# A four-mixer layer on one core: another order for the same instructions

## The chip, the core and the metric

The kernel runs on one core of a Trainium2 chip. The metric is the device time of one execution in microseconds (us), lower is better. The core has five engines that run their own queues in order: PE (matmuls, with its weight loads shown as PEld), DVE and ACT (vector and scalar work), POOL (a third elementwise engine) and SP, which issues the transfers.

## The reference, cut to what matters

One layer over 2048 positions of width 1024: normalise, project to four mixers, run them side by side, project back, normalise and add.

```python
h = _rmsnorm(x, pre_norm_w)
proj = jnp.einsum('btd,de->bte', h, w_in)              # 1024 -> 4120
p_gdn, p_rwkv, p_sc, p_gla = _split(proj, [...])
y_gdn = _gated_deltanet(p_gdn, ...)                    # chunks of 64, a triangular solve per chunk
y_rwkv = _rwkv7(p_rwkv, ...)                           # a recurrence over positions
y_sc = _short_conv(p_sc, sc_conv_w)
y_gla = _gla(p_gla, ...)                               # chunks of 64, a decayed state
y = jnp.concatenate([y_gdn, y_rwkv, y_sc, y_gla], axis=-1)
out = jnp.einsum('bte,ed->btd', y, w_out)
x = x + _rmsnorm(out, post_norm_w)
```

Each of the deltanet, rwkv and gla has four heads and a state that is carried from one chunk of 64 positions to the next, so their chunks follow one another.

## The kernel before, in words

The sequence is cut into 4 blocks of 512 positions. For each block the main thread `projections` multiplies 31 weight tiles (128 columns each) with the normalised input. A tile takes 24 matmuls of 128x512, since weights and input are held as a high and a low part, into one of two PSUM banks called pp; an epilogue on ACT, DVE and POOL reads the bank. The order of tiles in a block is deltanet, rwkv, short convolution, gla. After block 4 the same thread does the output projection, `out_proj`.

The mixers run beside it as further threads, Python generators that issue a few operations and then yield:

- `prepare` makes, for each block, the deltanet's gates and norms, then the matrices of each tile of 128 positions; the same for rwkv (`rwkv_prep`, twice per block, once per pair of heads, with a long run of DVE and ACT operations from L867 to L889, then `rwkv_mats`); then `gla_prep`.
- `inverses` inverts the 64x64 triangular matrices, 8 chunk matrices at a time, 16 times in all. Each goes through levels: matmuls into the bank psi, a masked product W on DVE (L591), matmuls with Yb, a sum X (L596), a transpose Y (L598), block-diagonal copies Yb (L583).
- `chains` carries the states: `gdn_chain`, `rwkv_chain` and `gla`, with PSUM banks psc and psa; after a tile, `norm` normalises its output (L1069 to L1081) and a thread `put` gates and stores it.
- `stats` and `front` normalise the next block's input; `load_out` loads the output weights.

**How the order comes about.** There are two steps. First the program order: `weave` (L227) keeps a planner's time `self.t`, which only matmuls advance, and each thread's due time. A number that a thread yields is a delay from the table `LAT`; a tuple is an event to wait for. The main thread steps until `BEAT` (1.5 us of planner's time) has passed since the mixers last had their turn, then every thread that is due steps, again and again until none is due. Second, the tile scheduler takes the program and orders each engine's queue: it runs a model of the machine and hands each engine, whenever it is free in that model, the ready instruction that comes first by program position. `tc.high_priority(offset=n)` moves the operations inside it n positions ahead for that choice; it is used for weight loads, for the input's high and low parts, and for the epilogues of projections (400 each). It changes no dependence. On the chip each queue then runs in the order fixed so, whatever the real durations are.

Buffers tie the blocks together: the deltanet projections of a block wait for the deltanet outputs of the block before (`yield "G", blk - 1`), and the rwkv projections for the rwkv outputs (L1381):

```python
more[0] = (("R", blk - 1) if blk else None,) + more[0][1:]
```

Of the kernel before, what the change touches and what calls it, by code (L numbers as in the profile page):

```python
# [19 lines left out]
P = 128  # L20
# [105 lines left out]
class Ring:  # L126
# [6 lines left out]
    def __call__(self):  # L133
# [31 lines left out]
FPRIO = 400  # L165

BEAT = 1.5
RG = 4
BANKS = {"pp": 2, "psa": 3, "psi": 1, "psc": 2}

LAT = {"gates": 6.0, "ipre": 2.0, "gates2": 1.0, "norms": 3.2, "chan": 0.9, "pool": 1.38, "decay": 2.6, "mats": 2.2, "inv0": 1.0, "inv1": 2.2,
       "invr": 0.8, "chA": 1.0, "chB": 0.7, "chC": 0.48, "rpre": 5.0, "rchan": 4.5, "gpre": 3.0, "gA": 1.1,
       "gB": 0.62, "out": 8.0, "front": 0.3, "rdec": 0.6, "fdone": 2.0, "wo0": 2.8, "wo1": 1.4, "bonus": 2.5}
# [12 lines left out]


class K:
    def __init__(self, tc, a, out):
        self.tc, self.nc, self.a, self.out = tc, tc.nc, a, out  # L190
        self.t, self.left, self.ev, self.threads = 0.0, 0.0, {}, []

# [10 lines left out]
    def thread(self, gen, prio):  # L203
        self.threads.append([prio, 0.0, None, gen])
        self.threads.sort(key=lambda th: th[0])
# [11 lines left out]
    def step(self, th):  # L217

        y = next(th[3], "end")
        if y == "end":  # L220
            self.threads.remove(th)
        elif isinstance(y, tuple):
            th[2] = y
        else:
            th[1] = self.t + y

    def weave(self):  # L227

        while self.threads:
            main = self.threads[-1]
            ready = [th for th in self.threads if th[0] < 99 and self.can(th)]
            if main[0] == 99 and self.can(main) and (not ready or self.t - self.left < BEAT):
                self.step(main)
            elif ready:
                while ready:
                    for th in ready:
                        self.step(th)
                    ready = [th for th in self.threads if th[0] < 99 and self.can(th)]  # L240
                self.left = self.t
            else:
                if not any(self.can(th) for th in self.threads):
                    w = [th[1] for th in self.threads if th[2] is None]
                    assert w, [(th[0], th[2]) for th in self.threads]
                    self.t = max(self.t, min(w))
# [311 lines left out]
    def inverse(self, Bh, Bl, n):  # L558
# [9 lines left out]
        for c in range(2):  # L568
            nc.vector.tensor_copy(Bb[hs(c), :, hs(c)], Bh[hs(c)])

# [4 lines left out]
        Y = self.R16["Y"]()  # L575
        nc.vector.tensor_tensor(Y, Bh, m4(self.n1t), ALU.mult)
        nc.vector.tensor_tensor(Y, Y, I16, ALU.add)
        X = self.R16["X"]()
        nc.vector.transpose(X, Y)
        def diag():  # L580
            Yb = self.Rbd["Yb"]()
            for c in range(2):
                nc.vector.tensor_copy(Yb[hs(c), :, hs(c)], Y[hs(c)])  # L583
            return Yb
        Yb = diag()
        yield LAT["ipre"]
        for lv in range(4):
            ps = self.psi()
            mmb(ps, Bb, X)
            W = self.R16["W"]()  # L590
            nc.vector.tensor_tensor(W, v(ps), m4(self.lev[lv]), ALU.mult)  # L591
            yield LAT["inv0"]
            ps = self.psi()
            mmb(ps, Yb, W)
            X2 = self.R16["X"]()
            nc.vector.tensor_tensor(X2, v(ps), X, ALU.add)  # L596
            X = X2
            nc.vector.transpose(Y, X)  # L598
            Yb = diag()
            yield LAT["inv0"] if lv == 3 else LAT["inv1"]  # L600
        ps = self.psi()
        mmb(ps, Bb, X)
        W = self.R16["W"]()
        nc.vector.tensor_tensor(W, v(ps), m4(self.lev[4]), ALU.mult)
        yield LAT["inv0"]
# [6 lines left out]
        X2 = self.R16["X"]()  # L612
        nc.vector.tensor_tensor(X2, v(px), X, ALU.add)
        nc.vector.tensor_tensor(Y, py, Y, ALU.add)
        X = X2

        T = self.R16["X"]()
        nc.vector.tensor_tensor(T, I16, X, ALU.subtract)
        yield LAT["invr"]
# [6 lines left out]
        R = self.R16["W"]()  # L626
        nc.vector.tensor_tensor(R, T, v(ps), ALU.subtract)
        yield LAT["inv0"]
# [6 lines left out]
        Yf = self.R["Yf"]()  # L635
        nc.vector.tensor_tensor(v(Yf), v(ps), Y, ALU.add)
        return v(Yf)
# [209 lines left out]
    def rwkv_prep(self, blk):  # L847
# [10 lines left out]
        for pr in range(2):  # L858
# [14 lines left out]
            nc.vector.memset(e[:, :, 0:1], 1.0)  # L873
            nc.scalar.activation(e[:, :, 1:65], c3(G), AF.Exp)
            ev = e.rearrange("p (a c) t -> p a c t", c=2)
            en, ak = self.t2(), self.t2()
# [5 lines left out]
            nc.vector.scalar_tensor_tensor(ak, av, 1.0, kk, ALU.add, ALU.mult)  # L882
            nc.vector.tensor_tensor(slot(bks, 0), c4(ak), c4(en), ALU.mult)
            nc.scalar.activation(av, av, AF.Identity, scale=self.d[:, 17 + pr:18 + pr], bias=self.d[:, 13 + pr:14 + pr])
            nc.vector.tensor_tensor(k_, k_, m3(av), ALU.mult)
            nc.vector.scalar_tensor_tensor(m3(add[:, pr, :]), r_, self.pcol("rk", pr), k_, ALU.mult, ALU.mult)
            nc.vector.tensor_tensor(k_, k_, m3(en), ALU.mult)
            nc.vector.tensor_tensor(slot(ars, 1), slot(ars, 1), ev[:, :, :, 1:65], ALU.mult)
# [82 lines left out]
    def gdn_chain(self, tt, m, Y):  # L971
# [5 lines left out]
        for cp in range(2):  # L977
# [3 lines left out]
            for pr in range(2):  # L981
                self.mm(pA[:, P * pr:P * pr + P], g["kqc"][pr][:, c, :], S[:, pr, :], start=True, stop=True)
            nc.vector.tensor_tensor(h4(D)[q], h4(pA[:, 0:256])[q], bc(g["ne1"])[q], ALU.mult)
            nc.vector.tensor_tensor(D[q], D[q], m["vT"][q], ALU.add)
            nc.vector.tensor_tensor(h4(t)[qn], h4(pA[:, 0:256])[qn], bc(g["e1s"])[qn], ALU.mult)
            n = 8 * cp + 2 * tt
            nc.vector.tensor_tensor(S, S, g["dec"][:, n:n + 2].unsqueeze(2).to_broadcast([P, 2, P]), ALU.mult)
            yield LAT["chA"]
# [4 lines left out]
            for hp in range(2):  # L993
                nc.scalar.copy(qh(w)[q, :, hp, :], pB[hs(hp), 0:P].rearrange("p (q d) -> p q d", q=2))  # L994
            yield LAT["chB"]
# [11 lines left out]
        for cp in range(2):  # L1007
            nc.vector.tensor_tensor(og[hs(cp)], t[hs(1 - cp)], pO[hs(1 - cp), 0:256], ALU.add)
        return og

    def add_state(self, S, pC):
        pv = pC[:, 0:P].rearrange("p (q d) -> p q d", q=2)
        for hp in range(2):
            sb = S[hs(hp), :, hs(hp)]
            self.nc.vector.tensor_tensor(sb, sb, pv[hs(hp)], ALU.add)

    def rwkv_chain(self, tt, m, Y):
# [11 lines left out]
        for cp in range(2):  # L1029
            c = 2 * tt + cp  # L1030
            q = hs(cp)
            for pr in range(2):
                self.mm(pAc[cp][:, P * pr:P * pr + P], r["AR"][pr][:, c, :], S[:, pr, :], start=False, stop=True, skip_group_check=True)
            nc.scalar.copy(D[q], pAc[cp][q])
            nc.vector.tensor_tensor(S, S, r["dec"][:, :, c:c + 1].to_broadcast([P, 2, P]), ALU.mult)
            yield LAT["chB"]
# [3 lines left out]
            for hp in range(2):  # L1040
                s = slice(4 * tt + hp, 4 * tt + hp + 3, 2)
                nc.vector.tensor_tensor(qh(uv[:, cp, :])[q, :, hp, :], pB[hs(hp), 0:P].rearrange("p (q d) -> p q d", q=2),  # L1042
                                        r["nkn"][hp == cp][hs(hp), s].unsqueeze(2).to_broadcast([64, 2, 64]), ALU.mult)
# [12 lines left out]
        for cp in range(2):  # L1056
            nc.scalar.copy(og[hs(cp)], pAc[cp][hs(1 - cp)])
        return og
# [165 lines left out]
    def gla_prep(self):  # L1224
# [7 lines left out]
        dec = self.R["ld"]()  # L1232
        nc.vector.tensor_copy(dec, c3(eb)[:, :, 63])
        nc.scalar.activation(en, G, AF.Exp, scale=-1.0 / 16)
        nc.vector.tensor_tensor(c3(ed), c3(G)[:, :, 63:64].to_broadcast([P, NC, 64]), c3(G), ALU.subtract)
        nc.scalar.activation(G, ed, AF.Exp, scale=1.0 / 16)
        nc.gpsimd.tensor_tensor(G, kf, G, ALU.mult)
        nc.vector.tensor_tensor(kf, kf, en, ALU.mult)
        L.update(ed=G, dec=dec)
# [9 lines left out]
    def gla(self, blk, tt):  # L1249
# [9 lines left out]
        ke, vt = kv[:, 0:P], kv[:, P:]  # L1259
        nc.vector.tensor_tensor(h4(at), h4(pa[:, 0:256]), self.incl.unsqueeze(1).to_broadcast([P, 4, 64]), ALU.mult)  # L1260
        pt = self.psa()
        for i, t in enumerate([L["ed"]] + L["v"]):
            self.tr(pt[:, i * P:(i + 1) * P], t[:, ts], self.ident)
        nc.scalar.copy(kv, pt[:, 0:3 * P])
        yield LAT["gA"]
# [11 lines left out]
        for cp in range(2):  # L1277
            c = 2 * tt + cp
            for h in range(4):
                self.mm(po[hs(cp), hs(h)], self.qbd[:, cp, h, :], self.Sl, start=False, stop=True, skip_group_check=True)  # L1280
            nc.vector.scalar_tensor_tensor(self.Sl, self.Sl, L["dec"][:, c:c + 1], pC[cp], ALU.mult, ALU.add)  # L1281
            if cp == 0:
# [5 lines left out]
        o = u1()  # L1288
        nc.scalar.copy(o, po[:, 0:256])
        self.norm(o, u1, EPS, False)  # L1290
# [144 lines left out]
```

## Time and profile before

| | |
|---|---|
| median of 3 runs | 1380.93 us (1374.62 to 1382.09) |
| profiled execution, time | 1382.66 us |
| profiled execution, span | 1380.9 us |
| instructions | 25696 |
| PE busy | 1286.0 us, 93% |
| PEld busy | 974.5 us, 71% |
| DVE busy | 966.9 us, 70% |
| ACT busy | 532.1 us, 39% |
| POOL busy | 357.1 us, 26% |

The span runs from the first to the last instruction; the profiled execution's own time holds 1.8 us more. Busy shares are means over stages that differ: the first 35 us load and split weights, the middle mixes projections with the four mixers, and from about 1265 us on only the output projection is left. Names such as W, Yb, psi or gu are the program's tiles, and L591 is line 591 of the kernel before. Matmuls overlap one another, so a row's mean duration is longer than the time from one matmul to the next.

### The profile page before, as it was taken

The numbers are of one execution on the slowest core, as the hardware profiler recorded it, in microseconds if no ns is written. First come the engines' busy times: TensorE is split into PE (matmuls) and PEld (weight loads), VectorE is DVE, ScalarE is ACT, GpSimd is POOL, SyncE is SP. The second block draws the span as 40 slices with busy tenths as digits, with TensorE's granted clock in tenths as the row PEclk, the third lists the DMA queues.
The fourth block names the chain that finished last, engine by engine and source line by source line (L and its number), as shares of the span: only waits on it lengthen the run. The fifth ranks groups of instructions, "written<-read, shape, count | busy, mean of one in ns | idle before, by whom it ended". The sixth has DMA issues, their size and how long they took to land. (4 is left out here: it accounts for less than half of the span.)

```text
span 1380.9 us, 25696 instructions
## 1 busy us (share of the span) xinstructions
PE 1286.0 (93%) x9928; PEld 974.5 (71%) x9928; DVE 966.9 (70%) x2194; ACT 532.1 (39%) x1165; POOL 357.1 (26%) x437
## 2 busy tenths in 40 slices
PE   5989988899999999999999899999998998999997
PEld 3767766667767777767677677676776776777886
DVE  5776697778886787688757894888669847643222
ACT  4653454235442441435524422453234234232221
POOL 5564443301121121111311211103112144232221
PEclk9999999999999999999999999999999998999999
DMA  7876554453244424453444333532444362233442
GB/s 278 272 253 228 206 176 145 142 167 121 92 139 136 155 93 151 140 177 123 139 145 137 123 126 130 165 125 93 146 134 142 117 213 87 93 111 100 150 151 99
DMA packets 98506, 204.47 MB, mean 148 GB/s; under 512 B 9152, under 2 KB 39248, under 8 KB 98384
## 3 DMA queue, kind: packets, MB, share of 16 engines
q1 hardware_dynamic: 98384, 202.83, 44.6%
q8 instruction: 78, 1.28, 0.4%
q14 instruction: 44, 0.36, 0.1%
HBM read 153.51 MB, written 49.28 MB: 147 GB/s over the span
## 5 line engine op out<-in xcount | busy, mean ns | idle before, releaser
L197 PE MATMUL pp<-hh,w 128*128 128x512 f32 (+1 forms) x2272 | 642.2, 408 | 7.9 <-ACT hh L432 4.0
L197 PEld LDWEIGHTS pp<-hh,w 128*128 128x128 f32 (+1 forms) x2272 | 413.0, 190 | 96.8 <-issue 5.1
L197 PE MATMUL pp<-hl,w 128*128 128x512 f32 (+1 forms) x1152 | 340.7, 408 | 2.0 <-POOL hl L433 2.0
L197 PEld LDWEIGHTS pp<-hl,w 128*128 128x128 f32 (+1 forms) x1152 | 209.3, 190 | 47.3 <-POOL hl L433 3.8
L350 POOL TENSOR_TENSOR w<-raw,w 128x512 fp32r<-128x512 f32 (+1 forms) x102 | 129.2, 1270 | 222.1 <-ACT w L349 121.6
L354 POOL TENSOR_TENSOR sm<-sm,mhalf 128x4 f32<-128x4 f32 (+1 forms) x64 | 59.7, 933 | 221.7 <-DVE sm L1077 196.0
L349 ACT CAST w<-raw 128x512 fp32r<-128x512 f32 (+1 forms) x102 | 60.4, 594 | 132.2 <-issue 60.9
L197 PE MATMUL pp<-woh,w 128*128 128x512 f32 x256 | 73.8, 409 | 0.0
L659 DVE SCALAR_TENSOR_TENSOR pq<-pq,par,pq 128x512 f32<-128x512 f32 x72 | 59.0, 819 | 14.7 <-ACT pq L656 12.3
L583 DVE COPY Yb<-Y 64x512 f16<-64x512 f16 x160 | 57.2, 358 | 2.2
L197 PEld LDWEIGHTS <-Yb 128*128 128x128 f16 x640 | 24.9, 99 | 44.5 <-issue 18.7
L197 PE MATMUL psi<-W,Yb 128*128 128x64 f16 x640 | 33.1, 196 | 23.5 <-DVE W L591 16.9
L197 PEld LDWEIGHTS pp<-woh,w 128*128 128x128 f32 x256 | 48.0, 193 | 9.5
L596 DVE TENSOR_TENSOR X<-psi,X 128x512 f16<-128x512 f32 x64 | 43.9, 686 | 9.6 <-PE psi L197 9.2
L197 PEld LDWEIGHTS <-Bb 128*128 128x128 f16 x768 | 29.6, 99 | 27.2 <-issue 21.6
L1368 DVE SCALAR_TENSOR_TENSOR pq<-pq,sm,x 128x512 f32<-128x512 f32 x32 | 24.0, 751 | 31.1 <-DMA x<-in_x 20.6
L598 DVE STREAM_TRANSPOSE Y<-X 128x512 f16<-128x512 f16 x64 | 45.2, 706 | 0.9
L1357 ACT ACTIVATE x<-pp 128x512 f32<-128x512 f32 x32 | 19.1, 598 | 68.8 <-PE pp L197 68.8
L591 DVE TENSOR_TENSOR W<-psi,c 128x512 f16<-128x512 f32 x64 | 43.6, 682 | 1.7 <-PE psi L197 1.2
L197 PE MATMUL psi<-X,Bb 128*128 128x64 f16 x768 | 39.7, 195 | 4.1 <-DVE X L596 3.6
L994 ACT COPY gu<-psc 64x128 f32<-64x128 f32 x64 | 16.7, 260 | 59.0 <-PE psc L197 58.0
L1358 DVE TENSOR_TENSOR pq<-pp,lg 128x512 f32<-128x512 f32 x16 | 11.1, 691 | 36.2 <-ACT x L1357 36.2
(317 smaller groups left out, 2087.2 us busy)
## 6 DMA issues: line engine op xcount, KB each, us to landing
w<-parts SPq DMA_DIRECT2D x186, 512.0 KB, 3.3
parts<-w SPq DMA_DIRECT2D x62, 512.0 KB, 4.0
raw<-in_wt SPq DMA_DIRECT2D x62, 256.0 KB, 3.1
x<-in_x SPq DMA_DIRECT2D x56, 256.0 KB, 3.0
raw<-yd SPq DMA_DIRECT2D x32, 256.0 KB, 2.9
out<-pq SPq DMA_DIRECT2D x32, 256.0 KB, 2.1
x<-in_xt SPq DMA_DIRECT2D x24, 256.0 KB, 2.9
yd<-y SPq DMA_DIRECT2D x32, 128.0 KB, 2.0
```

What stands on the lines that cost most here:

```text
L197: return self.nc.tensor.matmul(out, w, x, **kw)
L349: self.nc.scalar.copy(hi, src)
L350: self.nc.gpsimd.tensor_tensor(lo, src, hi.bitcast(F32), ALU.subtract)
L354: self.nc.gpsimd.tensor_tensor(dst, x, self.mhalf[:, 0:x.shape[1]], ALU.pow)
L583: nc.vector.tensor_copy(Yb[hs(c), :, hs(c)], Y[hs(c)])
L591: nc.vector.tensor_tensor(W, v(ps), m4(self.lev[lv]), ALU.mult)
L596: nc.vector.tensor_tensor(X2, v(ps), X, ALU.add)
L598: nc.vector.transpose(Y, X)
L659: nc.vector.scalar_tensor_tensor(acc, p[:, i:i + BL], self.pcol("conv", 4 * ct + i), acc, ALU.mult, ALU.add)
L994: nc.scalar.copy(qh(w)[q, :, hp, :], pB[hs(hp), 0:P].rearrange("p (q d) -> p q d", q=2))
L1357: nc.scalar.activation(junk, ps[i], AF.Square, accum_out=ss[:, i:i + 1])
L1368: nc.vector.scalar_tensor_tensor(o, o, r, x, ALU.mult, ALU.add)
```

## The change

The same arithmetic is issued in another order.

- The tile scheduler uses its timeline model instead of its default one to order the queues (`schedule_with_timeline_sim=True`).
- A wrapper `Urgent` issues an operation with a priority offset of 800. `self.uv` wraps DVE and `self.ua` wraps ACT; the inverse's DVE operations, and the chains' DVE and ACT operations that lie on the states' way, go through them.
- `rwkv_prep` yields three times inside its run of operations (0.5 us each by the planner) and its closing delay falls from 5.0 to 1.0; `gla_prep` yields twice.
- In `weave`, a thread that has yielded a positive delay takes no second step in the same visit.

```diff
+URGENT = 800
-       "invr": 0.8, "chA": 1.0, "chB": 0.7, "chC": 0.48, "rpre": 5.0, "rchan": 4.5, "gpre": 3.0, "gA": 1.1,
+       "invr": 0.8, "chA": 1.0, "chB": 0.7, "chC": 0.48, "rpre": 1.0, "burst": 0.5, "rchan": 4.5, "gpre": 3.0, "gA": 1.1,
+class Urgent:
+    def __init__(self, tc, eng):
+        self.tc, self.eng = tc, eng
+    def __getattr__(self, name):
+        op = getattr(self.eng, name)
+        def f(*a, **kw):
+            with self.tc.high_priority(offset=URGENT):
+                return op(*a, **kw)
+        return f
+        self.uv, self.ua = Urgent(tc, tc.nc.vector), Urgent(tc, tc.nc.scalar)
 # step
             th[1] = self.t + y
+            if y > 0.0:
+                th[4] = self.visit
 # weave
             elif ready:
+                self.visit += 1
                 while ready:
                     for th in ready:
                         self.step(th)
-                    ready = [th for th in self.threads if th[0] < 99 and self.can(th)]
+                    ready = [th for th in self.threads if th[0] < 99 and self.can(th) and th[4] < self.visit]
 # inverse (all its DVE operations likewise)
-            nc.vector.tensor_tensor(W, v(ps), m4(self.lev[lv]), ALU.mult)
+            self.uv.tensor_tensor(W, v(ps), m4(self.lev[lv]), ALU.mult)
 # rwkv_prep
             nc.scalar.activation(e[:, :, 1:65], c3(G), AF.Exp)
+            yield LAT["burst"]
...
             nc.vector.tensor_tensor(slot(bks, 0), c4(ak), c4(en), ALU.mult)
+            yield LAT["burst"]
...
             nc.vector.scalar_tensor_tensor(m3(add[:, pr, :]), r_, self.pcol("rk", pr), k_, ALU.mult, ALU.mult)
+            yield LAT["burst"]
 # gdn_chain, rwkv_chain, add_state and gla (their operations on D, t, S, w, uv, og, at, kv, Sl, o likewise)
-            nc.vector.tensor_tensor(h4(D)[q], h4(pA[:, 0:256])[q], bc(g["ne1"])[q], ALU.mult)
+            self.uv.tensor_tensor(h4(D)[q], h4(pA[:, 0:256])[q], bc(g["ne1"])[q], ALU.mult)
-                nc.scalar.copy(qh(w)[q, :, hp, :], pB[hs(hp), 0:P].rearrange("p (q d) -> p q d", q=2))
+                self.ua.copy(qh(w)[q, :, hp, :], pB[hs(hp), 0:P].rearrange("p (q d) -> p q d", q=2))
 # gla_prep
         nc.vector.tensor_copy(dec, c3(eb)[:, :, 63])
+        yield LAT["burst"]
...
         nc.gpsimd.tensor_tensor(G, kf, G, ALU.mult)
+        yield LAT["burst"]
 # kernel
-    with tile.TileContext(nc) as tc:
+    with tile.TileContext(nc, schedule_with_timeline_sim=True) as tc:
```

## Rows read from the trace of the kernel before

**Rows 1.** Page, busy us (share of the span) by engine, and instructions.

```profile
PE 1286.0 (93%) x9928; PEld 974.5 (71%) x9928; DVE 966.9 (70%) x2194; ACT 532.1 (39%) x1165; POOL 357.1 (26%) x437
```

**Rows 2.** Stretches: length, PE, PEld, DVE, ACT, POOL, clock, DMA, GB/s.

```profile
0.00:35.00 35.00, 19.31 (x73) 13.42 (x74) 17.95 (x43) 17.20 (x36) 20.64 (x27) 1.00 0.80 280
175.00:210.00 35.00, 27.72 (x162) 20.91 (x160) 33.19 (x52) 17.17 (x29) 17.65 (x14) 0.90 0.49 170
...
245.00:280.00 35.00, 29.97 (x232) 22.64 (x232) 26.94 (x54) 10.25 (x21) 8.23 (x9) 0.90 0.47 159
1295.00:1330.00 35.00, 35.00 (x156) 28.98 (x155) 10.01 (x19) 8.81 (x22) 9.62 (x9) 1.00 0.44 147
1365.00:1381.00 16.00, 8.39 (x38) 6.60 (x36) 4.49 (x8) 1.38 (x4) 0.55 (x1) 0.87 0.30 106
```

**Rows 3.** Chain that ended last, in time: start us, us, what.

```profile
1276.35 97.06 PE pp L197 x428
```

**Rows 4.** Page, instruction groups: xcount, busy us, mean ns, idle before.

```profile
L197 PE MATMUL pp<-hh,w 128*128 128x512 f32 (+1 forms) x2272 | 642.2, 408 | 7.9 <-ACT hh L432 4.0
```

**Rows 5.** PE's waits, by what ended them: total us, times, longest.

```profile
PE psi L197 <- DVE W L591: 16.9, 11, 4.8
...
PE psc L197 <- DVE gu L984: 8.1, 11, 2.9
PE psa L201 <- DVE or L1081: 4.5, 4, 2.6
PE psi L197 <- DVE Yb L583: 4.3, 7, 0.9
...
PE psi L197 <- DVE X L596: 3.6, 5, 2.1
PE psa L197 <- DVE t L779: 3.4, 1, 3.4
PE psc L197 <- DVE UV L1042: 3.1, 5, 0.8
PE pp L197 <- DMA w<-parts: 2.4, 3, 1.2
```

**Rows 6.** Timeline, DVE and PE, 182 to 188.6: start us, us, instruction.

```profile
182.95 2.77 DVE L583 COPY Yb<-Y 64x512 f16<-64x512 f16 x2
185.75 0.69 DVE L896 TENSOR_REDUCE n<-t 128x8 f32<-128x512 f32 x1
186.36 1.22 DVE L871 TENSOR_TENSOR_SCAN t<-c,t 128x512 f32<-128x512 f16 x1
187.50 0.68 DVE L591 TENSOR_TENSOR W<-psi,c 128x512 f16<-128x512 f32 x1
...
188.24 0.58 PE L197 MATMUL psi<-W,Yb 128*128 128x64 f16 x8 [4.79 <-DVE W L591]
```

**Rows 7.** Groups of DVE by line, whole span.

```profile
L591 DVE TENSOR_TENSOR W<-psi,c 128x512 f16<-128x512 f32 x64 | 43.6, 682 | 1.7 <-PE psi L197 1.2
```

**Rows 8.** Cores: span and mean granted clock.

```profile
core 0: 1380.9 us, clock 0.979
```

**Rows 9.** Timeline, the operation L1077 twice and POOL beside the first.

```profile
242.34 1.30 POOL L1237 TENSOR_TENSOR lg<-lqk,lg 128x512 f32<-128x512 f32 x1
242.44 1.22 DVE L1077 TENSOR_SCALAR sm<-sm 128x4 f32<-128x4 f32 x1
...
678.52 0.16 DVE L1077 TENSOR_SCALAR sm<-sm 128x4 f32<-128x4 f32 x1
```

**Rows 10.** Timeline, ACT: rwkv chain's last copies, projections' first epilogues.

```profile
373.90 0.59 ACT L825 COPY pq<-pp 128x512 f32<-128x512 f32 x1
383.77 0.75 ACT L1057 COPY or<-psc 64x256 f32<-64x256 f32 x2 [3.75 <-PE psc L197]
...
660.02 0.74 ACT L1057 COPY or<-psc 64x256 f32<-64x256 f32 x2 [1.65 <-PE psc L197]
...
673.62 0.57 ACT L825 COPY pq<-pp 128x512 f32<-128x512 f32 x1
```

More of the change, by code (lines that the diff above doesn't have):

```diff
@@ L190, in __init__ @@
         self.tc, self.nc, self.a, self.out = tc, tc.nc, a, out
-        self.t, self.left, self.ev, self.threads = 0.0, 0.0, {}, []
+        self.uv, self.ua = Urgent(tc, tc.nc.vector), Urgent(tc, tc.nc.scalar)
+        self.t, self.left, self.visit, self.ev, self.threads = 0.0, 0.0, 0, {}, []
     def mm(self, out, w, x, **kw):
@@ L203, in thread @@
     def thread(self, gen, prio):
-        self.threads.append([prio, 0.0, None, gen])
+        self.threads.append([prio, 0.0, None, gen, 0])
         self.threads.sort(key=lambda th: th[0])
@@ L568, in inverse @@
         for c in range(2):
-            nc.vector.tensor_copy(Bb[hs(c), :, hs(c)], Bh[hs(c)])
+            self.uv.tensor_copy(Bb[hs(c), :, hs(c)], Bh[hs(c)])
         def mmb(ps, l, r):
@@ L575, in inverse @@
         Y = self.R16["Y"]()
-        nc.vector.tensor_tensor(Y, Bh, m4(self.n1t), ALU.mult)
-        nc.vector.tensor_tensor(Y, Y, I16, ALU.add)
+        self.uv.tensor_tensor(Y, Bh, m4(self.n1t), ALU.mult)
+        self.uv.tensor_tensor(Y, Y, I16, ALU.add)
         X = self.R16["X"]()
-        nc.vector.transpose(X, Y)
+        self.uv.transpose(X, Y)
         def diag():
@@ L582, in diag @@
             for c in range(2):
-                nc.vector.tensor_copy(Yb[hs(c), :, hs(c)], Y[hs(c)])
+                self.uv.tensor_copy(Yb[hs(c), :, hs(c)], Y[hs(c)])
             return Yb
@@ L595, in inverse @@
             X2 = self.R16["X"]()
-            nc.vector.tensor_tensor(X2, v(ps), X, ALU.add)
+            self.uv.tensor_tensor(X2, v(ps), X, ALU.add)
             X = X2
-            nc.vector.transpose(Y, X)
+            self.uv.transpose(Y, X)
             Yb = diag()
@@ L603, in inverse @@
         W = self.R16["W"]()
-        nc.vector.tensor_tensor(W, v(ps), m4(self.lev[4]), ALU.mult)
+        self.uv.tensor_tensor(W, v(ps), m4(self.lev[4]), ALU.mult)
         yield LAT["inv0"]
@@ L612, in inverse @@
         X2 = self.R16["X"]()
-        nc.vector.tensor_tensor(X2, v(px), X, ALU.add)
-        nc.vector.tensor_tensor(Y, py, Y, ALU.add)
+        self.uv.tensor_tensor(X2, v(px), X, ALU.add)
+        self.uv.tensor_tensor(Y, py, Y, ALU.add)
         X = X2
         T = self.R16["X"]()
-        nc.vector.tensor_tensor(T, I16, X, ALU.subtract)
+        self.uv.tensor_tensor(T, I16, X, ALU.subtract)
         yield LAT["invr"]
@@ L626, in inverse @@
         R = self.R16["W"]()
-        nc.vector.tensor_tensor(R, T, v(ps), ALU.subtract)
+        self.uv.tensor_tensor(R, T, v(ps), ALU.subtract)
         yield LAT["inv0"]
@@ L635, in inverse @@
         Yf = self.R["Yf"]()
-        nc.vector.tensor_tensor(v(Yf), v(ps), Y, ALU.add)
+        self.uv.tensor_tensor(v(Yf), v(ps), Y, ALU.add)
         return v(Yf)
@@ L982, in gdn_chain @@
                 self.mm(pA[:, P * pr:P * pr + P], g["kqc"][pr][:, c, :], S[:, pr, :], start=True, stop=True)
-            nc.vector.tensor_tensor(h4(D)[q], h4(pA[:, 0:256])[q], bc(g["ne1"])[q], ALU.mult)
-            nc.vector.tensor_tensor(D[q], D[q], m["vT"][q], ALU.add)
-            nc.vector.tensor_tensor(h4(t)[qn], h4(pA[:, 0:256])[qn], bc(g["e1s"])[qn], ALU.mult)
+            self.uv.tensor_tensor(h4(D)[q], h4(pA[:, 0:256])[q], bc(g["ne1"])[q], ALU.mult)
+            self.uv.tensor_tensor(D[q], D[q], m["vT"][q], ALU.add)
+            self.uv.tensor_tensor(h4(t)[qn], h4(pA[:, 0:256])[qn], bc(g["e1s"])[qn], ALU.mult)
             n = 8 * cp + 2 * tt
-            nc.vector.tensor_tensor(S, S, g["dec"][:, n:n + 2].unsqueeze(2).to_broadcast([P, 2, P]), ALU.mult)
+            self.uv.tensor_tensor(S, S, g["dec"][:, n:n + 2].unsqueeze(2).to_broadcast([P, 2, P]), ALU.mult)
             yield LAT["chA"]
@@ L1007, in gdn_chain @@
         for cp in range(2):
-            nc.vector.tensor_tensor(og[hs(cp)], t[hs(1 - cp)], pO[hs(1 - cp), 0:256], ALU.add)
+            self.uv.tensor_tensor(og[hs(cp)], t[hs(1 - cp)], pO[hs(1 - cp), 0:256], ALU.add)
         return og
@@ L1014, in add_state @@
             sb = S[hs(hp), :, hs(hp)]
-            self.nc.vector.tensor_tensor(sb, sb, pv[hs(hp)], ALU.add)
+            self.uv.tensor_tensor(sb, sb, pv[hs(hp)], ALU.add)
     def rwkv_chain(self, tt, m, Y):
@@ L1033, in rwkv_chain @@
                 self.mm(pAc[cp][:, P * pr:P * pr + P], r["AR"][pr][:, c, :], S[:, pr, :], start=False, stop=True, skip_group_check=True)
-            nc.scalar.copy(D[q], pAc[cp][q])
-            nc.vector.tensor_tensor(S, S, r["dec"][:, :, c:c + 1].to_broadcast([P, 2, P]), ALU.mult)
+            self.ua.copy(D[q], pAc[cp][q])
+            self.uv.tensor_tensor(S, S, r["dec"][:, :, c:c + 1].to_broadcast([P, 2, P]), ALU.mult)
             yield LAT["chB"]
@@ L1041, in rwkv_chain @@
                 s = slice(4 * tt + hp, 4 * tt + hp + 3, 2)
-                nc.vector.tensor_tensor(qh(uv[:, cp, :])[q, :, hp, :], pB[hs(hp), 0:P].rearrange("p (q d) -> p q d", q=2),
+                self.uv.tensor_tensor(qh(uv[:, cp, :])[q, :, hp, :], pB[hs(hp), 0:P].rearrange("p (q d) -> p q d", q=2),
                                         r["nkn"][hp == cp][hs(hp), s].unsqueeze(2).to_broadcast([64, 2, 64]), ALU.mult)
@@ L1056, in rwkv_chain @@
         for cp in range(2):
-            nc.scalar.copy(og[hs(cp)], pAc[cp][hs(1 - cp)])
+            self.ua.copy(og[hs(cp)], pAc[cp][hs(1 - cp)])
         return og
@@ L1259, in gla @@
         ke, vt = kv[:, 0:P], kv[:, P:]
-        nc.vector.tensor_tensor(h4(at), h4(pa[:, 0:256]), self.incl.unsqueeze(1).to_broadcast([P, 4, 64]), ALU.mult)
+        self.uv.tensor_tensor(h4(at), h4(pa[:, 0:256]), self.incl.unsqueeze(1).to_broadcast([P, 4, 64]), ALU.mult)
         pt = self.psa()
@@ L1263, in gla @@
             self.tr(pt[:, i * P:(i + 1) * P], t[:, ts], self.ident)
-        nc.scalar.copy(kv, pt[:, 0:3 * P])
+        self.ua.copy(kv, pt[:, 0:3 * P])
         yield LAT["gA"]
@@ L1280, in gla @@
                 self.mm(po[hs(cp), hs(h)], self.qbd[:, cp, h, :], self.Sl, start=False, stop=True, skip_group_check=True)
-            nc.vector.scalar_tensor_tensor(self.Sl, self.Sl, L["dec"][:, c:c + 1], pC[cp], ALU.mult, ALU.add)
+            self.uv.scalar_tensor_tensor(self.Sl, self.Sl, L["dec"][:, c:c + 1], pC[cp], ALU.mult, ALU.add)
             if cp == 0:
@@ L1288, in gla @@
         o = u1()
-        nc.scalar.copy(o, po[:, 0:256])
+        self.ua.copy(o, po[:, 0:256])
         self.norm(o, u1, EPS, False)
```

## Prediction

> **What bounds the kernel now.** Read the page's busy times first [rows 1]: PE 93%, DVE 70%, ACT 39%, POOL 26%. PE is the bound, and its visible idle time is 1380.9 - 1286.0 = 94.9 us. Next come the stretches [rows 2]. The first 35 us hold 35 - 19.31 = 15.7 us of that idle time (the first block's loads) and the last 16 us hold 7.6 us (the last output tile); the change touches neither. 71.6 us remain, spread over the middle. Then the chain of work that ended last [rows 3]: one piece of 428 projection matmuls in 97.06 us, 0.227 us each. A single one is shown as 0.408 us long [rows 4], so each matmul's shown end covers up to 0.408 - 0.227 = 0.18 us in which PE could already have begun the next, and each visible wait is that much longer than it looks. Then PE's waits [rows 5]: the long ones are for DVE operations of the mixers, namely the inverse's W, Yb and X, the deltanet chain's gu, and rwkv's UV. Last, one wait in detail [rows 6]: PE stands for 4.79 us at a matmul that needs W, while DVE runs a copy of Yb (2.77 us for two), a reduction of rwkv's preparation (0.69) and its scan (1.22), and W only after them. Over the whole run DVE idles just 1.7 us before its 64 W operations [rows 7]. W nearly always queues behind other DVE work; it seldom finds DVE waiting for it.
>
> How far down the time can go depends on what is taken for a full PE. The Trainium skill ("Perfetto Trace Analysis", Identifying the Most-Contended Engine) holds that matmul busy time says little of how near PE is to its limit, and that weight loading's share is the better measure. By the trace, weight loads are busy 28.98 of 35 us where PE is dense, 0.83, against 974.5 us in all [rows 1, 2]. By that page the floor is an estimated 974.5 / 0.83 = 1177 us and some 200 us of PE's time is slack; by the busy row it is 95 us. The sum below uses the visible waits alone.
>
> **The change part by part.** No matmul, transfer or elementwise operation is added or removed. All parts move instructions in the engines' queues, so each price is a wait removed or made.
>
> *Priority for the mixers' operations.* The inverse's DVE operations and the chains' DVE and ACT operations go ahead of preparations and projection epilogues that the scheduler holds ready at the same moment. The five waits of this kind in [rows 5] sum to 16.9 + 8.1 + 4.3 + 3.6 + 3.1 = 36.0 us in 39 waits; with 0.18 us hidden in each, 43.1 us. An operation that goes first still waits for the rest of what is running, half of some 0.7 us [rows 7], 0.35 us: 39 x 0.35 = 13.7 us stays, and 29.4 us could go. Not all will, since the order is fixed beforehand by modelled durations. In [rows 6], W could have started at 185.75 where the reduction did, 1.75 us earlier, 0.4 of the wait. I take 0.7, midway between this and all: -20.6 us. Bounds: 0 and -43.1.
>
> *What is put back.* The norms of the chains' outputs (L1077 to L1081) get no priority and now stand behind the urgent operations. PE waits 4.5 us for them today [rows 5]; I let this double: +4.5 us, bounds 0 and +9. The epilogues that read projection banks stand back too. A bank takes 24 matmuls, 24 x 0.227 = 5.4 us, to fill, and there are two, so an epilogue that comes later by two or three operations of 0.7 us is covered: 0. Without that cover it would be 0.7 us for each operation put ahead.
>
> *Preparations split.* One block half of rwkv's preparation issues its ten DVE operations from L871 to L889 in one go, and gla's preparation its four; now they come in four and three pieces, and the pause behind rwkv's shrinks from 5.0 to 1.0 in the kernel's own planner, with three pauses of 0.5 between pieces. This lets mixer operations in between, which the first term counts already. Of its own it can take the wait for t at L779 (3.4 us, a preparation behind others) [rows 5].
>
> *Another model for the order.* No row of before shows how the other model orders. It has two kinds of wait to work on that priority doesn't touch: 2.4 us for transfers and the 3.4 us at L779 [rows 5]. I take both, -5.8 us, for the split and the model together. Bounds: the visible idle time that the first term leaves, 71.6 - 36.0 = -35.6 us; on the other side an order that fits worse and doubles the five waits, +36.
>
> *One step of a thread per visit.* It adds nothing while the projections can't run, since the next visit follows at once; while they can, a thread that would have taken two steps in one visit waits for the next. I take 0; the case where it costs is a rival below.
>
> *The clock.* PE's mean granted clock is 0.979 [rows 8], a loss of 29 us over the span. From 175 to 280 us it is 0.90, a mix of the levels 2.4 and 1.2 GHz, in three stretches of 35 us, in the first and last of which PE was busy for 27.7 and 30.0 us [rows 2]: 105 x 0.10 = 10.5 us lost. In 1295 to 1330, PE without a gap, it is 1.00. If 0.7 of the waits go there, so does about 0.7 of that loss: -7 us, bounds 0 and -29.
>
> Sum: -20.6 + 4.5 - 5.8 - 7 = -28.9 us. The profiled execution took 1382.66 us (span 1380.9, 1.8 us around it), so 1354 us; it lies 0.1% above the median of 1380.93, for which I make no allowance. That is 1.9% faster.
>
> **The rivals.** *Most waits go.* Priority takes the five waits whole (43.1) and the better order the remaining visible idle time (35.6): 1382.7 - 78.7 = 1304 us. For it: 36 of 71.6 us has this one cause. Against it: DVE runs 33.19 of 35 us around the wait of [rows 6] [rows 2], where order alone can't make room.
>
> *No change.* DVE's durations follow what POOL does, so an order fixed beforehand misses them. The scalar operation L1077 on 128x4 took 1.22 us while POOL ran a 1.30 us operation beside it, and 0.16 us elsewhere [rows 9]. With 1 us of such stretch the urgent operation is late whatever its rank, and the first and last terms fall away: -5.8 + 4.5 = -1.3, 1381 us. The Trainium skill ("GPSIMD Engine Reference", Specifications) says that POOL's interfaces to SBUF are shared with VectorE and contended; the rows agree.
>
> *Slower.* Place: the rwkv projections of the next block may not be issued before the rwkv outputs of the block before are through (L1381). PE time between the chain's last output copies and the first epilogue of those projections is short or negative today: 383.77 against 373.90 us, and 660.02 + 0.74 = 660.76 against 673.62, a margin of 12.9 us [rows 10]. The chain has 24 steps per block, each now at most one per visit, and a visit lets the projections run for up to 1.5 of the planner's us. Above 12.9 / 24 = 0.5 us more per step it decides: the chain ends behind the margin and PE runs out of projections. At 10 us per boundary and three boundaries: +30 us, 1413 us. For it: the margin. Against it: those operations also gain priority, and when the projections are blocked the visits follow at once.
>
> **How the numbers follow.** The forecast has 0.40 (its own range 1330 to 1373), most waits go 0.22, no change 0.14, slower 0.24. A measurement of this kernel can tell about 0.5% from no change, 1374 to 1388 us. So faster is 0.40 + 0.22 = 0.62, same 0.14, slower 0.24. Range: the lower end reaches past the large gain, to 1296; of the slower case, whose size is open, it takes the smaller half, to 1404, which leaves some 0.08 below and 0.12 above. By the bounds of all terms it could be -43 - 36 - 29 = -108 at best and +36 + 9 at worst.
>
> **What would show it.** In the changed trace, PE's waits for W, gu, Yb, X and UV should fall from 36 us to under 18, DVE should still have next to no idle time before W, and PE's visible idle time should fall to some 70 us. The wait for the norms (L1081's counterpart) should grow to 5 to 9 us. The granted clock from 175 to 280 us should rise above 0.95. Waits for projection banks should stay absent. The prediction is wrong on the slow side if projection matmuls thin out at block boundaries, at 350 to 380 us and 290 us after, while PE has only chain work; it is wrong on the fast side if PE's share exceeds 96%.

## The result, and the profile after

The changed kernel takes 1594.51 us (median of 4 runs, 1590.56 to 1594.71), the kernel before 1379.53 us in the same comparison: a ratio of 1.156, 95% interval 1.152 to 1.160. It is 215 us slower, far outside the range of 1296 to 1404 us.

The page's busy times, as in [rows 1], then the page's rows of PE's busy tenths and granted clock in 40 slices of 39.8 us:

```profile
PE 1378.3 (87%) x9928; PEld 1068.4 (67%) x9928; DVE 966.7 (61%) x2194; ACT 542.4 (34%) x1171; POOL 350.8 (22%) x437
...
PE   6989987997599968995889968995899956998998
...
PEclk9999996997599986996799978996799955997999
```

The work is the same: DVE is busy for 966.7 us as before, to a fifth of a microsecond, and the counts of PE, DVE and POOL are equal. What has changed is when it is done. PE's visible idle time is 1592.9 - 1378.3 = 214.6 us, against 94.9 us before, and most of it lies in holes, stretches without a projection matmul, of which each kind recurs about every 345 us. PE's busy time has grown as well, by 92.3 us for the same 9928 matmuls: those that are not projections cover 483 us instead of 394. The eight longest holes between 228 and 1351 us, 21 to 79 us each, hold 380 us; the kernel before has no stretch over 8.1 us without a projection matmul.

Five stretches of the changed kernel, columns as in [rows 2]; the first and the last stand beside the stretches of the same kind there:

```profile
175.00:210.00 35.00, 35.00 (x214) 27.68 (x213) 13.94 (x32) 11.82 (x23) 16.64 (x15) 1.00 0.76 263
...
392.00:440.00 48.00, 29.15 (x343) 22.85 (x343) 43.79 (x124) 8.80 (x23) 5.55 (x8) 0.60 0.05 15
580.00:612.00 32.00, 19.43 (x158) 14.65 (x158) 29.58 (x65) 19.65 (x42) 8.02 (x7) 0.55 0.00 1
730.00:783.00 53.00, 32.09 (x317) 24.05 (x317) 41.42 (x117) 17.22 (x39) 6.00 (x8) 0.56 0.02 6
...
1520.00:1555.00 35.00, 35.00 (x157) 28.93 (x157) 11.97 (x23) 8.35 (x20) 11.07 (x11) 1.00 0.45 144
```

And three of them again for the projections alone, that is, for the instructions on the tile pp (PE, PEld, DVE, ACT, then clock, DMA share and GB/s of the whole core):

```profile
392.00:440.00 48.00, 0.00 (x0) 0.00 (x0) 0.00 (x0) 1.16 (x2) 0.60 0.05 15
580.00:612.00 32.00, 0.00 (x0) 0.00 (x0) 0.00 (x0) 0.00 (x0) 0.55 0.00 1
730.00:783.00 53.00, 0.00 (x0) 0.00 (x0) 0.00 (x0) 0.95 (x2) 0.56 0.02 6
```

Read them together. From 175 to 210 us PE is full and DVE has 13.94 us of work, where before DVE had 33.19 [rows 2]: PE is at projections and the mixers hardly move. In the holes it is the other way round. Not one projection matmul is issued for 32 to 53 us, DVE is busy for 41.42 of 53 us and up to 43.79 of 48, almost no weights are moved (1 to 15 GB/s), and PE has only the mixers' small matmuls, at a granted clock of 0.55 to 0.60. Work that used to overlap now takes turns: first projections, then mixers. The low clock is part of a hole's price: one of the inverse's steps of eight matmuls took 0.61 us in a hole (at 240.37 us), where it took 0.41 at 126.86, among projections. How much of the loss the clock makes was not separated.

What a hole ends with differs. Lines of ACT and PE at the end of the one from 391 us, then of the one from 575 us:

```profile
438.77 0.69 ACT L848 ACTIVATE pq<-pp,dpar 128x512 f32<-128x512 f32 x1 [0.81 <-DVE AR L852]
...
441.26 2.08 PE L215 MATMUL pp<-hh,w 128*128 128x512 f32 x4
```

```profile
614.43 1.28 ACT L454 CAST hh<-x 128x512 fp32r<-128x512 f32 x2 [0.41 <-DVE x L448]
...
615.33 1.97 PE L215 MATMUL pp<-hh,w 128*64 128x512 f32 x4
```

In the first, no epilogue reads a pp bank until rwkv's, L848, starts at 438.77; the holes from 724 and 1074 us end in the same way (782.05 and 1134.27). In the second, the next block's input, hh, comes first, as in the holes from 229 and 925 us (259.70 and 961.98). What held that epilogue and that input was not followed further back.

PE's waits, columns as in [rows 5]; all operations that go through the new wrapper carry its line, L201, and L215 is the old L197:

```profile
PE psi L215 <- DVE X L201: 42.9, 31, 5.0
PE psi L215 <- DVE Yb L201: 34.5, 17, 3.7
PE psi L215 <- DVE W L201: 14.6, 9, 2.9
...
PE psc L215 <- DVE UV L201: 10.9, 12, 2.0
PE psc L215 <- DVE gu L201: 10.8, 6, 3.4
```

The five waits that the priority was to remove sum to 113.7 us, against 36.0 in [rows 5]. As the wrapper puts all its operations on one line, the new rows of W and X take in two small ones of the kernel before that the 36.0 us leave out; with them the like sum before is 38.4 us:

```profile
PE psi L197 <- DVE W L604: 1.9, 3, 1.1
...
PE psi L197 <- DVE X L579: 0.5, 1, 0.5
```

Last, one step of the same inverse in both timelines (start us, us, instruction). The kernel before:

```profile
106.36 0.41 PE L197 MATMUL psi<-X,Bb 128*128 128x64 f16 x8
...
106.60 2.09 PE L197 MATMUL pp<-hh,w 128*128 128x512 f32 x8
106.81 0.69 DVE L591 TENSOR_TENSOR W<-psi,c 128x512 f16<-128x512 f32 x1 [0.23 <-PE psi L197]
...
108.54 0.41 PE L197 MATMUL psi<-W,Yb 128*128 128x64 f16 x8
```

The changed kernel:

```profile
126.86 0.41 PE L215 MATMUL psi<-X,Bb 128*128 128x64 f16 x8
...
127.31 0.69 DVE L201 TENSOR_TENSOR W<-psi,c 128x512 f16<-128x512 f32 x1 [0.91 <-PE psi L215]
127.33 1.17 PE L215 MATMUL pp<-hh,w 128*128 128x512 f32 x4
128.34 1.08 PE L215 MATMUL pp<-hl,w 128*128 128x512 f32 x4
129.26 1.98 PE L215 MATMUL pp<-hh,w 128*128 128x512 f32 x8
...
131.07 1.07 PE L215 MATMUL pp<-hl,w 128*128 128x512 f32 x4
131.98 0.39 PE L215 MATMUL pp<-hh,w 128*128 128x512 f32 x1
132.21 0.41 PE L215 MATMUL psi<-W,Yb 128*128 128x64 f16 x8
```

Before, W is ready at 107.50 and its matmul starts 1.0 us later, with 8 projection matmuls between the two steps of the inverse. After, W is ready at 128.00 and its matmul starts 4.2 us later, with 4 + 4 + 8 + 4 + 1 = 21 projection matmuls between the two steps. Over all 80 steps of this kind the median delay is 0.32 us before and 2.16 us after. Before, 8 projection matmuls is the commonest number between the steps (41 of 80); after, there are none in 38 of them, and 16 to 25, median 21, in 28. PE is never idle in the step shown, so PE's list of waits does not show this delay. DVE's list does in part: before UV, in the rwkv chain, DVE waits for PE 40.8 us in all, against 11.9:

```profile
DVE UV L1042 <- PE psc L197: 11.9, 10, 1.8
```

```profile
DVE UV L201 <- PE psc L215: 40.8, 18, 5.3
```

The lag that such delays build up is worked off in the holes.

### The profile page after: what moved, and what is told of

Read it like the earlier page. It is cut to its first block, busy times and chain, and to the rows that moved or that the text cites. A ratio compares the mean times of both kernels' runs of the same rounds, so it can differ in the third digit from the quotient of the medians.

```text
span 1592.9 us, 25731 instructions
## 1 busy us (share of the span) xinstructions
PE 1378.3 (87%) x9928; PEld 1068.4 (67%) x9928; DVE 966.7 (61%) x2194; ACT 542.4 (34%) x1171; POOL 350.8 (22%) x437
## 4 chain that ended last, share of the span: by engine, by line
PE 65%; DVE 22%; ACT 4%; issue 4%; DMA 3%; POOL 2%; SPq 0%; ACTq 0%; POOLq 0%; DVEq 0%
PE pp L215 51%; PE psc L215 6%; PE psa L215 4%; PE psi L215 2%; PE psa L219 2%; DVE Y L201 2%; DVE X L201 2%; DVE W L201 1%; DMA x<-in_x 1%; DVE x L448 1%; DVE Yb L201 1%; DVE Sr L201 1%; DVE gu L201 1%; DVE M L967 1%; DVE rB L971 1%
## 5 line engine op out<-in xcount | busy, mean ns | idle before, releaser
L215 PE MATMUL pp<-hh,w 128*128 128x512 f32 (+1 forms) x2272 | 624.8, 403 | 10.3 <-ACT pq L848 3.3
L215 PEld LDWEIGHTS pp<-hh,w 128*128 128x128 f32 (+1 forms) x2272 | 420.1, 190 | 105.4 <-ACT pq L848 3.9
L215 PE MATMUL pp<-hl,w 128*128 128x512 f32 (+1 forms) x1152 | 333.7, 403 | 3.6 <-DVE hl L455 2.8
L215 PEld LDWEIGHTS pp<-hl,w 128*128 128x128 f32 (+1 forms) x1152 | 215.9, 191 | 53.9 <-DVE hl L455 6.2
L215 PE MATMUL psi<-X,Bb 128*128 128x64 f16 x768 | 46.4, 211 | 43.1 <-DVE X L201 42.9
L201 DVE TENSOR_TENSOR X<-psi,X 128x512 f16<-128x512 f32 x80 | 54.9, 687 | 40.5 <-PE psi L215 39.8
L215 PE MATMUL psi<-W,Yb 128*128 128x64 f16 x640 | 39.5, 213 | 45.7 <-DVE Yb L201 34.5
L215 PEld LDWEIGHTS <-Bb 128*128 128x128 f16 x768 | 38.3, 110 | 60.6 <-issue 50.6
L215 PE MATMUL pp<-woh,w 128*128 128x512 f32 x256 | 71.1, 407 | 4.2 <-ACT w L371 2.9
L215 PEld LDWEIGHTS <-Yb 128*128 128x128 f16 x640 | 30.1, 110 | 63.3 <-DVE Yb L201 42.1
L215 PEld LDWEIGHTS pp<-woh,w 128*128 128x128 f32 x256 | 49.5, 196 | 15.4 <-ACT w L371 3.3
L201 DVE TENSOR_TENSOR W<-psi,c 128x512 f16<-128x512 f32 x80 | 54.5, 681 | 6.5 <-PE psi L215 6.0
L201 DVE COPY Yb<-Y 64x512 f16<-64x512 f16 x160 | 47.0, 294 | 1.7
L201 DVE STREAM_TRANSPOSE Y<-X 128x512 f16<-128x512 f16 x64 | 45.2, 707 | 1.1
L215 PE MATMUL psa<-AR,BK 64*128 64x128 f32 x256 | 41.4, 366 | 3.0 <-DVE AR L913 1.6
L201 DVE TENSOR_TENSOR UV<-psc,kn 64x128 f32<-64x128 f32 x64 | 18.4, 287 | 41.7 <-PE psc L215 40.8
L215 PE MATMUL psc<-UV,M 128*64 128x64 f32 (+1 forms) x512 | 36.9, 265 | 4.5 <-DVE UV L201 2.7
L215 PEld LDWEIGHTS psa<-AR,BK 64*128 64x128 f32 x256 | 34.5, 255 | 9.1 <-issue 3.2
```

What stands on the lines that cost most here:

```text
L201: return op(*a, **kw)
L215: return self.nc.tensor.matmul(out, w, x, **kw)
```

## Experiments

All ratios are to the kernel before, timed on the same chip in the same comparison.

### The changed kernel with the default model

```diff
-    with tile.TileContext(nc, schedule_with_timeline_sim=True) as tc:
+    with tile.TileContext(nc) as tc:
```

> The changed kernel, but ordered by the default model. Theory A (the timeline model alone makes the loss: in its order the projections run ahead of the mixers and then stand at the block boundaries): 1345 to 1385 us, PE never without projection matmuls for over 20 us before the output projection, clock above 0.97. Theory B (priority or the rule of one step per visit holds the mixers back): 1560 to 1620 us, with the same empty stretches.

Measured: 1384.39 us, ratio 1.0056 (1.0035 to 1.0076), clock 0.981, and no stretch over 8 us without a projection matmul. Theory A holds, at the upper edge of its range. Everything else in the change together is worth half a per cent, on the wrong side. PE's five waits here:

```profile
PE psc L215 <- DVE gu L201: 18.2, 19, 2.3
PE psi L215 <- DVE W L201: 12.8, 20, 1.7
...
PE psi L215 <- DVE X L201: 4.9, 6, 1.7
...
PE psc L215 <- DVE UV L201: 3.0, 6, 0.8
...
PE psi L215 <- DVE Yb L201: 1.5, 2, 0.9
```

They sum to 40.4 us, no less than the 38.4 of the like rows before; their longest is 2.3 us instead of 4.8, and there are more of them for W and gu.

### The timeline model as the only change

```diff
 # the kernel before
-    with tile.TileContext(nc) as tc:
+    with tile.TileContext(nc, schedule_with_timeline_sim=True) as tc:
```

> The kernel before, with the timeline model as the only change. Theory A: 1560 to 1620 us and stretches of 40 us and more without a projection matmul at each block boundary. Theory B: 1360 to 1400 us, none such.

Measured: 1600.01 us, ratio 1.162 (1.158 to 1.166). The model alone makes the whole loss. Stretches for pp alone, as above:

```profile
392.00:440.00 48.00, 0.00 (x0) 0.00 (x0) 0.00 (x0) 1.17 (x2) 0.57 0.06 15
727.00:777.00 50.00, 0.00 (x0) 0.00 (x0) 0.00 (x0) 0.00 (x0) 0.57 0.03 12
1072.00:1122.00 50.00, 0.00 (x0) 0.00 (x0) 0.00 (x0) 0.00 (x0) 0.60 0.03 12
1264.00:1360.00 96.00, 0.00 (x0) 0.00 (x0) 0.00 (x0) 0.00 (x0) 0.57 0.10 28
```

The holes stand at the same places, block for block, and the one behind the last block's projections, ahead of the output projection, is the longest.

### The change without the priority, and without the rule of one step per visit

```diff
-        self.uv, self.ua = Urgent(tc, tc.nc.vector), Urgent(tc, tc.nc.scalar)
+        self.uv, self.ua = tc.nc.vector, tc.nc.scalar
```

> The changed kernel without the priority of the mixers' operations. Theory A: 1580 to 1640 us, as the priority then can only help or do nothing. Theory B with the priority as the culprit: under 1450 us.

Measured: 1597.09 us, ratio 1.159 (1.155 to 1.164).

```diff
-                    ready = [th for th in self.threads if th[0] < 99 and self.can(th) and th[4] < self.visit]
+                    ready = [th for th in self.threads if th[0] < 99 and self.can(th)]
```

> The changed kernel in which a thread may again take several steps in one visit. Theory A: 1570 to 1610 us. Theory B with this rule as the culprit: under 1450 us, since the mixers then keep up.

Measured: 1590.31 us, ratio 1.154 (1.150 to 1.159). Both lie in Theory A's ranges. Neither part is the cause, and neither matters beside the model.

### Projections pinned in PE's queue, with either model

The pin orders the first matmul of each group behind the PE instruction that stands before it in the program. It adds no wait on data.

```diff
                 for k in ks:
-                    self.mm(ps[0:w.shape[2]], w[:, k, :], h[:, 4 * i + k, :], start=(i + q + k == 0),
-                            stop=(last and k == 3 and q + 1 == len(pairs)))
+                    ins = self.mm(ps[0:w.shape[2]], w[:, k, :], h[:, 4 * i + k, :], start=(i + q + k == 0),
+                                  stop=(last and k == 3 and q + 1 == len(pairs)))
+                    if k == ks[0]:
+                        self.tc.keep_in_program_order(ins)
 # out_proj likewise
```

> The changed kernel, timeline model included, with the first matmul of every group of projection matmuls pinned behind the PE instruction that stands before it in the program, so that projections can't overtake the mixers in PE's queue. Theory A1 (the loss is projections overtaking the mixers): below 1450 us and no stretch over 20 us without a projection matmul. Theory A2 (the timeline model orders DVE and ACT badly, and PE waits for that): still above 1550 us.

> Control for the pinned run: the same pins, but the default model. If the pins alone cost something (projections may not fill a gap in PE's queue), 1400 to 1460 us, and the pinned run with the timeline model was held up by the pins, not by the model. If they cost nothing, 1375 to 1395 us, and some 70 us of the timeline model's loss lie in DVE's and ACT's order.

Measured: with the timeline model 1458.11 us, ratio 1.059 (1.057 to 1.061); with the default model 1441.75 us, ratio 1.048 (1.044 to 1.053). The first misses the bound of 1450 us that A1 had set, and it keeps holes of its own; the control says why. The stretches for pp alone, timeline model and then default model:

```profile
370.00:413.00 43.00, 0.00 (x0) 0.00 (x0) 0.00 (x0) 1.01 (x2) 0.64 0.05 17
```

```profile
366.00:403.00 37.00, 0.00 (x0) 0.00 (x0) 0.00 (x0) 0.18 (x1) 0.63 0.06 18
```

The program itself has a hole here (where the gla chain of the first block and the rwkv chain before it are issued), and the default model normally fills it by moving projections. Pinned, both models show it. With overtaking forbidden, the timeline model costs 1458.11 - 1441.75 = 16 us; with overtaking allowed it cost 1594.5 - 1384.4 = 210 us (two comparisons, their kernels before 2.6 us apart). So some nine tenths of its loss need projections that overtake the mixers in PE's queue. That the order of DVE and ACT has only the rest is shown no further than this: the pinned runs have holes of their own, in which a worse order of DVE and ACT could cost less than elsewhere. The pins are no remedy: the pinned kernel with the default model is 4.8% slower than the kernel before, and some 4% slower than the same kernel without pins (1384.39 us).

### Priority for the mixers' matmuls too

```diff
     def mm(self, out, w, x, **kw):
...
-        return self.nc.tensor.matmul(out, w, x, **kw)
+        if self.main:                      # set by proj and out_proj around their own matmuls
+            return self.nc.tensor.matmul(out, w, x, **kw)
+        with self.tc.high_priority(offset=URGENT):
+            return self.nc.tensor.matmul(out, w, x, **kw)
 # tr likewise, always with the priority
```

> The changed kernel in which the mixers' matmuls and transposes get the priority of 800 too. Theory B1 (the timeline model gives PE's queue its next matmuls some us before PE reaches them, so a mixer's matmul that is not ready then is passed by whatever its rank): 1575 to 1610 us. Theory B2 (projections win by rank): under 1480 us.

Measured: 1646.79 us, ratio 1.195 (1.190 to 1.201). Rank, by 800 positions, is not what the mixers' matmuls lack. That it got 3% worse was expected by neither theory, and its reason is open.

### A projection matmul that takes longer

```diff
-                    self.mm(ps[0:w.shape[2]], w[:, k, :], h[:, 4 * i + k, :], start=(i + q + k == 0),
+                    self.mm(ps[0:w.shape[2]], w[:, k, :].bitcast(F32), h[:, 4 * i + k, :].bitcast(F32), start=(i + q + k == 0),
```

> The changed kernel with each projection matmul in plain fp32, some four times as long; the planner counts it so. A look at how far ahead PE's queue is filled. If by a number of instructions (some 20 projection matmuls): the wait from W's end to the matmul on it, 2 us in the median and 4 in the upper tenth now, grows to 8 to 16 us. If by a time of some 4 us: it stays at 2 to 5 us.

Measured: 3423.27 us in a single run. This kernel does not compute the layer; only the order and the times of its queues are read. The trace shows each plain fp32 matmul as two instructions (12968 on PE, not 9928), so an instruction is some twice as long here rather than four times, 7.03 / 16 = 0.44 us. The kernel's planner counts such a matmul as four times as long, so the program order differs too. One step of an inverse in the timeline:

```profile
1029.01 0.40 PE L215 MATMUL psi<-X,Bb 128*128 128x64 f16 x8
1029.24 1.96 PE L215 MATMUL pp<-hl,w 128*128 128x512 f32 x4
1029.44 0.69 DVE L201 TENSOR_TENSOR W<-psi,c 128x512 f16<-128x512 f32 x1 [7.65 <-PE psi L215]
1031.04 7.03 PE L215 MATMUL pp<-hh,w 128*128 128x512 f32 x16
...
1037.91 0.40 PE L215 MATMUL psi<-W,Yb 128*128 128x64 f16 x8
```

W is ready at 1030.13, its matmul starts 7.8 us later, and 4 + 16 = 20 projection instructions lie between the two steps. In the changed kernel it was 21, in 4.2 us. The step is typical: in 67 of the 80 there are 18 to 22 projection instructions, median 20, and the median delay over all 80 is 7.77 us, just under the 8 to 16 us expected for a fixed number and well above the 2 to 5 us for a fixed time. Instructions twice as long, the same number of them, nearly twice the delay: on the chip some 20 recorded PE instructions stand ahead of a mixer's next step, and not the work of a fixed time. Two things stay open. The 20 instructions are only 10 of the program's matmuls, against 21 in the changed kernel; and what the model itself takes a matmul to last is on no record, so a fixed time in the model's own reckoning is not ruled out.

### The other parts, each alone on the kernel before

Priority alone (the wrapper, without the other edits):

> The kernel before with the priority of the mixers' operations as the only change. The prediction's first term right: 1350 to 1360 us and PE's waits for W, gu, Yb, X and UV under 18 us in sum. Rival (the scheduler knows of the priority and moves PE's matmuls forward with it, so that the waits stay): 1372 to 1392 us and a sum of 30 to 45 us.

Measured: 1380.43 us, ratio 1.0035 (1.0011 to 1.0059). PE's waits for the mixers and the norms:

```profile
PE psc L215 <- DVE gu L201: 8.7, 13, 1.6
PE psi L215 <- DVE W L201: 8.7, 16, 2.7
PE psa L219 <- DVE or L1103: 7.4, 4, 3.5
PE psc L215 <- DVE UV L201: 6.2, 8, 1.5
...
PE psi L215 <- DVE X L201: 2.8, 5, 0.8
...
PE psi L215 <- DVE Yb L201: 1.5, 2, 0.9
```

The five sum to 27.9 us, against 38.4 in the like rows before; the wait for the norms rises by 2.9 us. The sum is neither under the 18 us of the forecast nor quite in the rival's 30 to 45; the time is the rival's, and none is gained.

Split preparations alone (three and two more yields, the pause 5.0 to 1.0):

> The kernel before with the split preparations and their shorter pause as the only change. By the prediction 1375 to 1380 us; as the carrier of the small loss seen under the default model, 1384 to 1392 us.

Measured: 1370.77 us, ratio 0.9954 (0.9938 to 0.997), some 6 us faster than before and better than the 1375 to 1380 us expected: the largest gain of any part, and the fastest kernel of this study, ahead of both the kernel before and the changed one.

One step per visit alone:

> The kernel before with one step of a thread per visit as the only change. By the prediction's main case 1374 to 1384 us; by its slower rival (the rwkv chain ends too late and the projections run dry at the block boundaries) 1400 us and more.

Measured: 1374.62 us, ratio 0.9978 (0.9962 to 0.9994), within the half per cent and within the main case's range. No boundary runs dry.

Both of these together, without priority and with the default model:

> The changed kernel without the timeline model and without the priority: split preparations and one step per visit. If the two small gains add (0.46% and 0.22%): 1366 to 1370 us, ratio 0.990 to 0.995. If they overlap: 1370 to 1376 us.

Measured: 1379.61 us, ratio 1.0009 (0.9989 to 1.0029). That lies above both expected ranges: the two do not add, and the gain of the split is gone. Differences of half a per cent among these orders belong to the whole order and not to a part.

## Why the prediction was wrong

The step that failed is the term "Another model for the order": -5.8 us, with bounds of -35.6 and +36. Alone the model costs 16.2% of 1377 us, 223 us. The upper bound took a worse order to mean that the five waits on DVE double. It left out that the order decides how far one kind of work runs ahead of another. The row that the bound should have come from is the whole of the overlap: DVE's 966.9 us of work [rows 1] stand beside projections only as long as the two are mixed.

What the runs showed in its place: under the timeline model, where projections are at hand, a mixer's matmul mostly comes some 20 PE instructions after the step before it. The inverses and chains are long rows of such steps, each waiting for the one before, so they slow down while the projections fill PE. At the block boundaries the projections stop, for a bank that no epilogue empties or for the next block's input, and PE and DVE work off the mixers alone: in the eight longest holes, 380 us, DVE is busy for 324 and PE for 234. That the model alone makes the loss was shown by switching it, either way; the overtaking by the pins and their control; that rank does not cure it by the urgent matmuls. The slower matmul shows the number of instructions ahead on the chip. How the model comes to fill the queue so far ahead was not looked into.

The other steps, one by one:

- *Priority*, -20.6 us: the mechanism works in part, since the longest wait for W falls from 4.8 to 2.7 us and the sum of like rows from 38.4 to 27.9. The size failed, and with it the step from waits to time, as the time did not fall. A likely reason, not shown: PE's order is made by the same model that knows of the priority, and a matmul that is expected earlier is placed earlier. Under the default model with all parts the waits are 40.4 us, more but shorter. The factor of 0.7 had no row behind its upper half. The rival *No change* had this outcome at 1381 us, where the change without the model took 1384.39; whether its mechanism is the reason, POOL stretching DVE's operations, was not tested.
- *What is put back*, +4.5 us: +2.9 us in the run with priority alone, right in kind and size.
- *Preparations split*: put at a part of -5.8 us together with the model; alone it is 6 us, but not through the wait for t at L779, which stays at 3.4 us in its trace. Which wait it removes is not settled.
- *One step per visit*, 0: alone within 0.5%, as said.
- *The clock*, -7 us: with the model it went the other way, from 0.979 to 0.878, with 0.55 to 0.60 in the holes and 1.00 where projections fill PE. With priority alone the three stretches from 175 to 280 us rose from 0.90 to 0.95, and no time came of it.
- *The slower rival* named the sign to look for, projections thinning out at the block boundaries from 350 us on and again later, and that sign appeared, from 361 us on. The place was right in part, since three of the holes end with rwkv's epilogue. Its cause, the rule of one step per visit, and its price of 30 us were both wrong; the right direction was luck.
- *The floor* of 1177 us by the weight loads and 200 us of slack were of no use here: the question was never how much PE could gain, but what it could lose.

## What to carry to other kernels

When a change lets something else decide the order, bound its loss by the overlap that the present order has, not by the waits that it leaves: ask which work could run ahead of which, and where it would then stop. A delay behind other useful work does not show in that engine's own list of waits; count the instructions between two steps of a chain in the timeline, and look for stretches in which the bound engine's main work is absent. Time the parts of a bundle alone before any of them is credited; here one switch held all of the loss, one edit alone had a gain of half a per cent that was gone beside another, and the rest were within half a per cent.

## What the runs showed of the hardware that was not expected

PE's granted clock was near its lower level, 1.2 GHz of 2.4, in stretches where PE was far from idle: 0.60 over 48 us with PE busy for 29.15 us of them, 0.55 over 32 us with 19.43, and 0.56 over 53 us with 32.09, on the mixers' small matmuls. At 27.72 of 35 us, with projections among them, it had been 0.90 [rows 2].
